# Stick-breaking scores without a mask product, and unsplit operands in 128-column products

## The chip, the cores and the metric

The kernel runs on one core of one Trainium2 chip. The metric is device time in microseconds of one execution; lower is better. A profile of one execution shows what each engine did: TensorE (PE, with its weight loads as PEld), VectorE (DVE), ScalarE (ACT), GpSimd (POOL) and the DMA queues issued from SP and ACT.

## What is computed

Two identical layers over 512 tokens of width 1024. Each layer norms the residual, projects it once, feeds four groups of heads, gates each group, concatenates, projects back, norms and adds. The two groups that matter here, cut to the core of the reference:

```python
def retention(q, k, v):                      # 4 heads of 128, chunks of 128
    q, k = apply_rope(q), apply_rope(k) * d ** -0.5
    scores = einsum('bcnhd,bcmhd->bchnm', qc, kc) * intra      # causal decay
    y_intra = einsum('bchnm,bcmhe->bcnhe', scores, vc)
    y = y_intra + y_inter                    # then a norm over each head
...
def stick_breaking(q, k, v):                 # 4 heads of 128, blocks of 128 queries
    logits = einsum('bthd,bshd->bhts', q_blk, k) * scale
    causal = key_pos[None, :] < q_pos[:, None]
    log_beta = log_sigmoid(logits)
    log_1mb = where(causal, log_sigmoid(-logits), 0.0)
    tail = cumsum(log_1mb, axis=3, reverse=True) - log_1mb
    w = where(causal, exp(log_beta + tail), 0.0)
    return einsum('bhts,bshd->bthd', w, v)
```

The other two groups are a state-space mixer (SSD) and a read of 256 memory tokens. Everything is float32.

## The kernel before

A product whose operands are float32 is written as three products in a reduced form (float32r): each operand is kept as a high part and a low part (a `Pair`: `h` and `l`, made by `split`, lines 287 to 290: a ScalarE copy that rounds, then a VectorE subtraction), and `mm3` (line 283) issues high by high, high by low and low by high into the same PSUM bank. Some products of the SSD group take float32 operands as they are, in one `mm` (lines 902 to 905, 919 and 936 to 945).

Weights come in blocks of 1 MB, are split on arrival (`w_prefetch`) and taken by the projections in a fixed order. The projections give banks of 128 features by 512 tokens (`proj_b`) or 128 tokens by 256 or 512 features (`proj_a`, `proj_v`). The work is written as a sequence of units; `defer` puts the later steps of a head some units behind, so that a head's chain of small steps runs beside the projections of later heads. The framework orders the instructions of each engine at compile time and places the semaphores; only the beginning (`start`) keeps the order in which it is written.

Stick-breaking, one head (`sb_head`, line 648): query and key are projected and split; for each of four blocks of 128 queries, t = 0 to 3, the scores against the first 128 (t + 1) keys are three split products and a fourth, bf16 product of an identity with a table of 0 and -1e30, which masks the keys at or after the query on the diagonal block (line 660; both bf16 tables lie in `b16`, filled at the end of `start`, and `b16` also feeds the warm-up products). Then, on the score tile `u`: absolute value, exponential and logarithm on ScalarE, a maximum and addition on VectorE, a reversed running sum on VectorE (the scan, line 666), a subtraction, and a last exponential, which gives the weights. `sb_head2` transposes the weights on TensorE (line 680) and splits them; `sb_head3` multiplies them with the values. The score tiles `w` lie in buffers of the tag "r" (9 of them); most others have the tag "s" (33) or "y" (16).

Retention, one head (`ret_head`, line 735): query and key are projected, rotated (`rope`) and split; for each chunk c of 128 keys the scores against the queries from that chunk on are one `mm3` of 512 - 128 c columns, which is split again, and the diagonal block of both parts is cleared by a GpSimd select (line 747). `ret_head2` multiplies them with the values, again with 512 - 128 c columns for chunk c. The values come from `ret_v`, one tile of 128 tokens each, shifted, scaled and split.

So for t = 0 in stick-breaking's scores, for the last j in its value product, and for the last c in both of retention's products the moving operand has 128 columns.

Of the kernel before, what the change touches and what calls it, by code (L numbers as in the profile page):

```python
# [16 lines left out]
P = 128  # L17
# [109 lines left out]
    return np.ascontiguousarray(t.T.reshape(KC, P, -1).transpose(1, 0, 2).reshape(P, -1))  # L127


CO = dict(ident=0, tri=128, ones=256, neg=384, cos=512, sin=1024, ginv=1536, reps=1552)  # L130
NCON = 1552 + 64
RP, RJ = 32, 16


def shape_constants():
    c = np.zeros((P, NCON), np.float32)
    i = np.arange(P)
    c[:, 0:128] = np.eye(P)
    c[:, 128:256] = i[:, None] <= i[None, :]
    c[:, 256:384] = 1.0  # L140
    c[:, 384:512] = np.where(i[None, :] >= i[:, None], NEG, 0.0)
    inv = np.float32(10000.0) ** (-np.arange(0, HD, 2, dtype=np.float32) / np.float32(HD))
    ang = (np.arange(SEQ, dtype=np.float32)[:, None] * inv[None, :].astype(np.float32)).T
    c[:, 512:1024] = np.concatenate([np.cos(ang), np.cos(ang)])
    c[:, 1024:1536] = np.concatenate([np.sin(ang), -np.sin(ang)])
# [3 lines left out]
    c[:, 1536:1552] = gi.reshape(NT, P, HEADS).transpose(1, 0, 2).reshape(P, 16)  # L149
    er = EPS * gam[None, :] ** (-2.0 * m[:, None])  # L150
    c[:RP, 1552:1616] = er.reshape(RP, RJ, HEADS).transpose(0, 2, 1).reshape(RP, HEADS * RJ)
    return c


# [16 lines left out]
class Builder:  # L171
# [4 lines left out]
    def __init__(self, tc, pools, args, taps=None):  # L176
        self.tc, self.nc = tc, tc.nc
        self.a = args
        self.taps = taps or {}
        self.fix, self.slots, self.small, self.wp, self.ps, self.dr = pools  # L180
        self.n = self.unit = 0
        self.todo, self.tanhs = [], []
        self.C = self.fixed(NCON + DEPTH * NPAR, F32, "consts")
        self.b16 = self.fixed(2 * P, BF16, "b16")
        self.onesr = self.fixed(P, F32R, "onesr")
        self.mhalf = self.fixed(RJ, F32, "mhalf")
        self.eps4 = self.fixed(RJ, F32, "eps4")
        self.nc.gpsimd.memset(self.mhalf[:], -0.5)
        self.nc.gpsimd.memset(self.eps4[:], EPS)

# [382 lines left out]
    def scaled_pair(self, b, scale):  # L573
# [2 lines left out]
        self.nc.vector.scalar_tensor_tensor(out=q.l, in0=b, scalar=scale, in1=q.hf, op0=ALU.mult, op1=ALU.subtract)  # L576
        return q

    @staticmethod
    def vcols(v, t, h):  # L580

        o = 256 * (t % 2) + HD * (h % 2)
        p = v[t // 2][h // 2]
        return p.h[:, o:o + HD], p.l[:, o:o + HD]
# [46 lines left out]
    def sb_v(self, l):  # L631
        nc = self.nc
        banks = self.proj_a(extra=SSD_H, turns=l == 0)
        if l:
            self.behind(self.turn[3], self.marks[1])
        first = [Pair(self), Pair(self)]
        u = self.tiny(32)
        uv = u.rearrange("p (h c) -> p c h", c=4)
        bias = self.par(l, "dtb", 0, 32).rearrange("p (h c) -> p c h", c=4)
        for t, b in enumerate(banks):  # L640
            p, c = first[t // 2], slice(256 * (t % 2), 256 * (t % 2) + 256)
            self.split(b[:, :256], p.h[:, c], p.l[:, c], p.hf[:, c])
            nc.vector.tensor_add(uv[:, t], b[:, 256:256 + SSD_H], bias[:, t])
        self.defer(1, self.dt_chain, l, u)
        second = [self.pair(b) for b in self.proj_a()]
        return [[first[i], second[i]] for i in range(2)]

    def sb_head(self, h, v):
        nc = self.nc
        q = self.scaled_pair(self.proj_b(), SCALE)  # L650
        k = self.pair(self.proj_b())
        w = [t[:, c] for t, c in self.packed([P * (t + 1) for t in range(NT)], lambda: self.buf(tag="r"))]
        for t in range(NT):
            n = P * (t + 1)
            ts = slice(P * t, P * t + P)
            b = self.mx()[:, :n]
            self.mm(b, q.h[:, ts], k.h[:, :n], True, False)
            self.mm(b, q.h[:, ts], k.l[:, :n], False, False)
            self.mm(b, q.l[:, ts], k.h[:, :n], False, False)
            self.mm(b[:, P * t:n], self.b16[:, 0:P], self.b16[:, P:2 * P], False, True)  # L660
            u = w[t]
            nc.scalar.activation(u, b, AF.Abs)
            self.act1(u, u, AF.Exp, scale=-1.0)
            self.act1(u, u, AF.Ln, bias=1.0)
            nc.vector.scalar_tensor_tensor(out=u, in0=b, scalar=0.0, in1=u, op0=ALU.max, op1=ALU.add)
            nc.vector.tensor_tensor_scan(out=u[:, ::-1], data0=u[:, ::-1], data1=u[:, ::-1], initial=0.0,
                                         op0=ALU.add, op1=ALU.bypass)
            nc.vector.tensor_sub(u, b, u)
            self.act1(u, u, AF.Exp)
        y = self.buf(tag="y")  # L670
        self.defer(4, self.sb_head2, h, v, w, y)
        return y

    def sb_head2(self, h, v, w, y):
        nc = self.nc
        wT = self.pairs_packed([SEQ - P * j for j in range(NT)])
        for j in range(NT):
            b = self.mx()
            for t in range(j, NT):
                nc.tensor.transpose(b[:, P * t:P * t + P], w[t][:, P * j:P * j + P], self.con("ident", P))  # L680
            self.split(b[:, P * j:], *wT[j])
        self.defer(2, self.sb_head3, h, v, wT, y)

    def sb_head3(self, h, v, wT, y):
# [24 lines left out]
    def rope(self, b):  # L709
        nc = self.nc  # L710
        cos, sin = self.con("cos", SEQ), self.con("sin", SEQ)
        A, B = self.buf(), self.buf()
        nc.vector.tensor_tensor(out=B[0:64], in0=b[64:128], in1=sin[64:128], op=ALU.mult)
        nc.vector.tensor_tensor(out=B[64:128], in0=b[0:64], in1=sin[0:64], op=ALU.mult)
        nc.vector.tensor_tensor(out=A, in0=b, in1=cos, op=ALU.mult)
        nc.vector.tensor_add(A, A, B)
        return self.pair(A)

    def row_rstd(self, row, eps):

# [14 lines left out]
    def ret_head(self, h, v):  # L735
        nc = self.nc
        q = self.rope(self.proj_b())
        k = self.rope(self.proj_b())
        sc = self.pairs_packed([SEQ - P * c for c in range(NT)])
        for c in range(NT):  # L740
            n = SEQ - P * c
            cs, ms = slice(P * c, SEQ), slice(P * c, P * c + P)
            b = self.mx()[:, :n]
            self.mm3(b, k.h[:, ms], k.l[:, ms], q.h[:, cs], q.l[:, cs], True, True)
            self.split(b, *sc[c])
            for d in (sc[c][0][:, :P], sc[c][1][:, :P]):
                nc.gpsimd.affine_select(out=d, in_=d, pattern=[[1, P]], compare_op=ALU.is_ge, fill=0.0, base=0, channel_multiplier=-1)  # L747
        y = self.buf(tag="y")
        self.defer(4, self.ret_head2, h, v, sc, y)
# [340 lines left out]
    def start(self):  # L1090
# [123 lines left out]
```

## Time and profile before

| | us |
|---|---|
| median of 3 runs | 954.48 (954.02 to 954.70) |
| the profiled execution | 954.77 |
| span of the profiled execution, first to last instruction | 953.0 |

The span is what the profile's views cover; 1.8 us of the execution lie around it. The granted TensorE clock was 0.998 of full speed over the span. How to read the rows that follow in the prediction: a group's row gives the line of the listing, the engine, the operation, output and inputs by the program's names, shapes and count, and after the bar the busy time in us and the mean of one in ns, then the idle time before. A row of the timeline gives start and duration in us; consecutive equal instructions are merged into one row with a count. TensorE's durations overlap, since products are pipelined. Most products lie in helper functions, so their line is 281 throughout, and the names of the operands tell them apart: `pj<-hTh,wh` is a projection, `mx<-s,s` an attention product, `mx<-b` the bf16 product.

### The profile page before, as it was taken

The numbers are of one execution on the slowest core, as the hardware profiler recorded it, in microseconds if no ns is written. First come the engines' busy times: TensorE is split into PE (matmuls) and PEld (weight loads), VectorE is DVE, ScalarE is ACT, GpSimd is POOL, SyncE is SP. The second block draws the span as 40 slices with busy tenths as digits, with TensorE's granted clock in tenths as the row PEclk, the third lists the DMA queues.
The fourth block names the chain that finished last, engine by engine and source line by source line (L and its number), as shares of the span: only waits on it lengthen the run. The fifth ranks groups of instructions, "written<-read, shape, count | busy, mean of one in ns | idle before, by whom it ended". The sixth has DMA issues, their size and how long they took to land.

```text
span 953.0 us, 12669 instructions
## 1 busy us (share of the span) xinstructions
PE 944.9 (99%) x4863; PEld 797.0 (84%) x4863; DVE 654.5 (69%) x1052; ACT 455.5 (48%) x840; POOL 102.0 (11%) x160
## 2 busy tenths in 40 slices
PE   9999999999999999999999999999999999999997
PEld 7998888888888888888899888888888888888885
DVE  5765577867878786854487465769777878767443
ACT  7544575543555342643465345655444544435341
POOL 1100000001231201100040000000003410102001
PEclk9999999999999999999999999999999999999999
DMA  9442211222232523344345221103222343223502
GB/s 339 144 159 86 89 45 45 89 89 89 97 103 100 166 89 122 123 154 144 117 172 189 90 89 62 72 1 133 85 76 80 137 140 127 99 75 116 193 29 88
DMA packets 26732, 105.76 MB, mean 111 GB/s; under 512 B 4144, under 2 KB 4400, under 8 KB 17456
## 3 DMA queue, kind: packets, MB, share of 16 engines
q10 hardware_dynamic: 10224, 73.44, 22.1%
q1 hardware_dynamic: 16448, 31.52, 10.0%
q8 instruction: 38, 0.62, 0.3%
q14 instruction: 22, 0.18, 0.1%
HBM read 100.63 MB, written 4.28 MB: 110 GB/s over the span
## 4 chain that ended last, share of the span: by engine, by line
PE 98%; DMA 1%; DVEq 0%; SPq 0%; ACT 0%; issue 0%; POOLq 0%; POOL 0%; ACTq 0%; DVE 0%
PE pj L281 72%; PE mx L281 23%; PE mx L680 1%; DMA mem<-memT 1%; PE mx L619 1%; PE mx L469 1%; PE mx L890 0%; PE mx L910 0%; DVEq L1210 0%; POOLq L1210 0%; ACT s L1058 0%; ACT s L512 0%; SPq L495 0%; SPq L343 0%; SPq L1094 0%
## 5 line engine op out<-in xcount | busy, mean ns | idle before, releaser
L281 PE MATMUL pj<-hTh,wh 128*128 128x512 f32 x704 | 277.1, 394 | 0.0
L281 PE MATMUL pj<-hTh,wl 128*128 128x512 f32 x704 | 276.5, 393 | 0.0
L281 PE MATMUL pj<-hTl,wh 128*128 128x512 f32 x704 | 276.3, 392 | 0.0
L290 DVE TENSOR_TENSOR wl<-raw,wh 128x1024 fp32r<-128x1024 f32 (+2 forms) x155 | 183.7, 1190 | 123.3 <-ACT wh L289 119.3
L289 ACT CAST wh<-raw 128x1024 fp32r<-128x1024 f32 (+2 forms) x155 | 157.9, 1024 | 191.8 <-PE pj L281 153.0
L281 PEld LDWEIGHTS pj<-hTh,wl 128*128 128x128 f32 x704 | 132.4, 188 | 26.8
L281 PEld LDWEIGHTS pj<-hTl,wh 128*128 128x128 f32 x704 | 132.4, 188 | 26.4
L281 PEld LDWEIGHTS pj<-hTh,wh 128*128 128x128 f32 x704 | 132.4, 188 | 26.2
L281 PE MATMUL pj<-wh,s 128*128 128x512 f32 x320 | 97.7, 391 | 0.0
L281 PE MATMUL mx<-s,s 128*128 128x128 f32 (+4 forms) x616 | 94.8, 309 | 0.0
L281 PEld LDWEIGHTS mx<-s,s 128*128 128x128 f32 (+1 forms) x616 | 84.5, 178 | 11.8 <-issue 2.4
L281 PE MATMUL mx<-wh,s 128*128 128x512 f32 x256 | 79.1, 389 | 0.0
L281 PEld LDWEIGHTS pj<-wh,s 128*128 128x128 f32 x320 | 59.7, 188 | 12.5
L747 POOL TENSOR_SCALAR_AFFINE_SELECT s<-s 128x128 fp32r<-128x128 f32 x64 | 20.5, 354 | 395.0 <-DVE s L290 395.0
L290 DVE TENSOR_TENSOR s<-mx,s 128x512 fp32r<-128x512 f32 (+2 forms) x86 | 41.8, 515 | 27.8 <-ACT s L289 27.8
L281 PE MATMUL pj<-wl,s 128*128 128x512 f32 x160 | 60.2, 390 | 0.0
L281 PEld LDWEIGHTS mx<-wh,s 128*128 128x128 f32 x256 | 48.1, 188 | 9.9
L290 DVE TENSOR_TENSOR s<-y,s 128x512 fp32r<-128x512 f32 x64 | 41.2, 686 | 19.7 <-ACT s L289 14.0
L289 ACT CAST s<-mx 128x512 fp32r<-128x512 f32 (+2 forms) x86 | 36.5, 456 | 37.0 <-PE mx L281 23.0
L289 ACT CAST s<-y 128x512 fp32r<-128x512 f32 x64 | 36.5, 617 | 29.4 <-PE mx L281 22.0
L281 PE MATMUL mx<-wl,s 128*128 128x512 f32 x128 | 49.6, 389 | 0.0
L281 PE MATMUL pj<-wl,hTh 128*128 128x256 f32 (+2 forms) x144 | 48.7, 338 | 0.0
(169 smaller groups left out, 1289.2 us busy)
## 6 DMA issues: line engine op xcount, KB each, us to landing
raw<-wts ACTq DMA_DIRECT2D x69, 1024.0 KB, 4.8
s<-x SPq DMA_DIRECT2D x24, 256.0 KB, 4.0
s<-acs SPq DMA_DIRECT2D x16, 256.0 KB, 6.4
raw<-wts SPq DMA_DIRECT2D x3, 1024.0 KB, 7.7
r<-row SPq DMA_DIRECT2D x12, 256.0 KB, 3.3
s<-acs SPq DMA_DIRECT2D x16, 128.0 KB, 5.9
x<-s SPq DMA_DIRECT2D x8, 256.0 KB, 2.0
out<-s SPq DMA_DIRECT2D x8, 256.0 KB, 2.0
```

The source lines that it names most:

```text
L281: return self.nc.tensor.matmul(out, lhsT, rhs, start=start, stop=stop)
L289: self.nc.scalar.copy(h, src)
L290: self.nc.vector.tensor_sub(l, src, hf)
L469: x = self.nc.tensor.transpose(b[:, P * j:P * j + P], hn[i][:, P * j:P * j + P], self.con("ident", P))
L619: nc.tensor.transpose(b[:, P * t:P * t + P], w[t // 2][:, o:o + P], self.con("ident", P))
L680: nc.tensor.transpose(b[:, P * t:P * t + P], w[t][:, P * j:P * j + P], self.con("ident", P))
L747: nc.gpsimd.affine_select(out=d, in_=d, pattern=[[1, P]], compare_op=ALU.is_ge, fill=0.0, base=0, channel_multiplier=-1)
```

## The change

1. The mask's product goes. The scan gets a constant table `run` (0 where a running sum starts, 1 elsewhere) as its first input, and multiplies the state by it before it adds: what lies at or after the query doesn't reach the sum. The weights of the diagonal block that should be zero are cleared by a GpSimd select after the last exponential.
2. Four 128-column triples a head become one product of float32 operands as they are. For that the first 128 columns of the scaled query and of the key are copied unsplit (`first_chunk`), the values' last chunk (`f` in `sb_v`) and the last transposed weights are kept unsplit, retention's rotated query and key are kept (`p.f`), and the last value tile of `ret_v` and the last score tile aren't split.
3. Buffers: the score tiles move to the tag "s", the last value tile of retention to "y". The constants get 384 columns more, and are loaded 3 and 12.6 tiles of 128 columns at a time instead of 4 and 8.6.

```diff
-            self.mm(b, q.h[:, ts], k.h[:, :n], True, False)
-            self.mm(b, q.h[:, ts], k.l[:, :n], False, False)
-            self.mm(b, q.l[:, ts], k.h[:, :n], False, False)
-            self.mm(b[:, P * t:n], self.b16[:, 0:P], self.b16[:, P:2 * P], False, True)
+            if t == 0:
+                self.mm(b, q.f, k.f, True, True)
+            else:
+                self.mm(b, q.h[:, ts], k.h[:, :n], True, False)
+                self.mm(b, q.h[:, ts], k.l[:, :n], False, False)
+                self.mm(b, q.l[:, ts], k.h[:, :n], False, True)
...
-            nc.vector.tensor_tensor_scan(out=u[:, ::-1], data0=u[:, ::-1], data1=u[:, ::-1], initial=0.0,
-                                         op0=ALU.add, op1=ALU.bypass)
+            nc.vector.tensor_tensor_scan(out=u[:, ::-1], data0=run[:, SEQ - n:][:, ::-1], data1=u[:, ::-1], initial=0.0,
+                                         op0=ALU.mult, op1=ALU.add)
             nc.vector.tensor_sub(u, b, u)
             self.act1(u, u, AF.Exp)
+            d = u[:, P * t:]
+            nc.gpsimd.affine_select(out=d, in_=d, pattern=[[-1, P]], compare_op=ALU.is_gt, fill=0.0, base=0, channel_multiplier=1)
...
+    def first_chunk(self, b, scale, out):
+        self.nc.scalar.activation(out, b[:, :P], AF.Copy, scale=scale)
+        return out
...
-        w = [t[:, c] for t, c in self.packed([P * (t + 1) for t in range(NT)], lambda: self.buf(tag="r"))]
+        w = [t[:, c] for t, c in self.packed([P * (t + 1) for t in range(NT)], self.buf)]
...
-            self.split(b[:, P * j:], *wT[j])
+            if j == NT - 1:
+                nc.scalar.copy(f, b[:, P * j:])
+            else:
+                self.split(b[:, P * j:], *wT[j])
...
-            self.mm3(b[:, c], *self.vcols(v, j, h), wT[j][0], wT[j][1], j == 0, j == NT - 1)
+            if j == NT - 1:
+                self.mm(b[:, c], v[2][:, HD * h:HD * h + HD], f, False, True)
+            else:
+                self.mm3(b[:, c], *self.vcols(v, j, h), wT[j][0], wT[j][1], j == 0, False)
...
-            vt = self.buf(tag="r")
+            vt = self.buf(tag="y" if t == NT - 1 else "r")
...
-            out.append(self.pair(vt))
+            out.append(vt if t == NT - 1 else self.pair(vt))
...
-            self.mm3(b, k.h[:, ms], k.l[:, ms], q.h[:, cs], q.l[:, cs], True, True)
-            self.split(b, *sc[c])
-            for d in (sc[c][0][:, :P], sc[c][1][:, :P]):
+            if c == NT - 1:
+                self.mm(b, k.f[:, ms], q.f[:, cs], True, True)
+                sc.append(k.f[:, :P])
+                nc.scalar.copy(sc[c], b)
+            else:
+                self.mm3(b, k.h[:, ms], k.l[:, ms], q.h[:, cs], q.l[:, cs], True, True)
+                self.split(b, *sc[c])
+            for d in (sc[c],) if c == NT - 1 else (sc[c][0][:, :P], sc[c][1][:, :P]):
...
-            self.mm3(b[:, P * c:], v[c].h[:, o], v[c].l[:, o], sc[c][0], sc[c][1], c == 0, c == NT - 1)
+            if c == NT - 1:
+                self.mm(b[:, P * c:], v[c][:, o], sc[c], False, True)
+            else:
+                self.mm3(b[:, P * c:], v[c].h[:, o], v[c].l[:, o], sc[c][0], sc[c][1], c == 0, False)
...
-        nc.sync.dma_start(self.C[:, 0:4 * P], self.a["consts"][:, 0:4 * P])
+        nc.sync.dma_start(self.C[:, 0:3 * P], self.a["consts"][:, 0:3 * P])
...
-        nc.sync.dma_start(self.C[:, 4 * P:NCON], self.a["consts"][:, 4 * P:NCON])
+        nc.sync.dma_start(self.C[:, 3 * P:NCON], self.a["consts"][:, 3 * P:NCON])
...
-        nc.vector.tensor_copy(self.b16[:, 0:P], self.con("ident", P))
-        nc.vector.tensor_copy(self.b16[:, P:2 * P], self.con("neg", P))
```

More of the change, by code (lines that the diff above doesn't have):

```diff
@@ L127, in features_first @@
     return np.ascontiguousarray(t.T.reshape(KC, P, -1).transpose(1, 0, 2).reshape(P, -1))
-CO = dict(ident=0, tri=128, ones=256, neg=384, cos=512, sin=1024, ginv=1536, reps=1552)
-NCON = 1552 + 64
+CO = dict(ident=0, tri=128, ones=256, run=384, cos=896, sin=1408, ginv=1920, reps=1936)
+NCON = 1936 + 64
 RP, RJ = 32, 16
@@ L140, in shape_constants @@
     c[:, 256:384] = 1.0
-    c[:, 384:512] = np.where(i[None, :] >= i[:, None], NEG, 0.0)
+    c[:, 384:896] = np.arange(512)[None, :] < 383 + i[:, None]
     inv = np.float32(10000.0) ** (-np.arange(0, HD, 2, dtype=np.float32) / np.float32(HD))
     ang = (np.arange(SEQ, dtype=np.float32)[:, None] * inv[None, :].astype(np.float32)).T
-    c[:, 512:1024] = np.concatenate([np.cos(ang), np.cos(ang)])
-    c[:, 1024:1536] = np.concatenate([np.sin(ang), -np.sin(ang)])
+    c[:, 896:1408] = np.concatenate([np.cos(ang), np.cos(ang)])
+    c[:, 1408:1920] = np.concatenate([np.sin(ang), -np.sin(ang)])
     gam = 1.0 - 2.0 ** (-5.0 - np.arange(HEADS, dtype=np.float64))
@@ L148, in shape_constants @@
     gi = gam[None, :] ** (-m[:, None]) * SCALE
-    c[:, 1536:1552] = gi.reshape(NT, P, HEADS).transpose(1, 0, 2).reshape(P, 16)
+    c[:, 1920:1936] = gi.reshape(NT, P, HEADS).transpose(1, 0, 2).reshape(P, 16)
     er = EPS * gam[None, :] ** (-2.0 * m[:, None])
-    c[:RP, 1552:1616] = er.reshape(RP, RJ, HEADS).transpose(0, 2, 1).reshape(RP, HEADS * RJ)
+    c[:RP, 1936:2000] = er.reshape(RP, RJ, HEADS).transpose(0, 2, 1).reshape(RP, HEADS * RJ)
     return c
@@ L183, in __init__ @@
         self.C = self.fixed(NCON + DEPTH * NPAR, F32, "consts")
+        self.mhalf = self.fixed(RJ, F32, "mhalf")
+        self.eps4 = self.fixed(RJ, F32, "eps4")
         self.b16 = self.fixed(2 * P, BF16, "b16")
         self.onesr = self.fixed(P, F32R, "onesr")
-        self.mhalf = self.fixed(RJ, F32, "mhalf")
-        self.eps4 = self.fixed(RJ, F32, "eps4")
         self.nc.gpsimd.memset(self.mhalf[:], -0.5)
@@ L644, in sb_v @@
         self.defer(1, self.dt_chain, l, u)
-        second = [self.pair(b) for b in self.proj_a()]
-        return [[first[i], second[i]] for i in range(2)]
+        f = self.buf(tag="r")
+        nc.scalar.copy(f[:, :256], banks[3][:, :256])
+        banks = self.proj_a()
+        second = [self.pair(b) for b in banks]
+        nc.scalar.copy(f[:, 256:], banks[1][:, 256:])
+        return [first[0], second[0]], [first[1], second[1]], f
     def sb_head(self, h, v):
         nc = self.nc
-        q = self.scaled_pair(self.proj_b(), SCALE)
-        k = self.pair(self.proj_b())
-        w = [t[:, c] for t, c in self.packed([P * (t + 1) for t in range(NT)], lambda: self.buf(tag="r"))]
+        f = self.buf(3 * P)
+        b = self.proj_b()
+        q = self.scaled_pair(b, SCALE)
+        q.f = self.first_chunk(b, SCALE, f[:, :P])
+        b = self.proj_b()
+        k = self.pair(b)
+        k.f = self.first_chunk(b, 1.0, f[:, P:2 * P])
+        w = [t[:, c] for t, c in self.packed([P * (t + 1) for t in range(NT)], self.buf)]
+        run = self.con("run", SEQ)
         for t in range(NT):
@@ L665, in sb_head, with sb_head2 @@
             nc.vector.scalar_tensor_tensor(out=u, in0=b, scalar=0.0, in1=u, op0=ALU.max, op1=ALU.add)
-            nc.vector.tensor_tensor_scan(out=u[:, ::-1], data0=u[:, ::-1], data1=u[:, ::-1], initial=0.0,
-                                         op0=ALU.add, op1=ALU.bypass)
+            nc.vector.tensor_tensor_scan(out=u[:, ::-1], data0=run[:, SEQ - n:][:, ::-1], data1=u[:, ::-1], initial=0.0,
+                                         op0=ALU.mult, op1=ALU.add)
             nc.vector.tensor_sub(u, b, u)
             self.act1(u, u, AF.Exp)
+            d = u[:, P * t:]
+            nc.gpsimd.affine_select(out=d, in_=d, pattern=[[-1, P]], compare_op=ALU.is_gt, fill=0.0, base=0, channel_multiplier=1)
         y = self.buf(tag="y")
-        self.defer(4, self.sb_head2, h, v, w, y)
+        self.defer(4, self.sb_head2, h, v, w, f[:, 2 * P:], y)
         return y
-    def sb_head2(self, h, v, w, y):
+    def sb_head2(self, h, v, w, f, y):
         nc = self.nc
-        wT = self.pairs_packed([SEQ - P * j for j in range(NT)])
+        wT = self.pairs_packed([SEQ - P * j for j in range(NT - 1)])
         for j in range(NT):
@@ L716, in rope @@
         nc.vector.tensor_add(A, A, B)
-        return self.pair(A)
+        p = self.pair(A)
+        p.f = A
+        return p
     def row_rstd(self, row, eps):
@@ L738, in ret_head @@
         k = self.rope(self.proj_b())
-        sc = self.pairs_packed([SEQ - P * c for c in range(NT)])
+        sc = self.pairs_packed([SEQ - P * c for c in range(NT - 1)])
         for c in range(NT):
```

4 lines of the change are left out of this document (2 added, 2 removed).

## The prediction

> **What bounds the kernel now.** I read the page's totals first, then the chain of work that ended last, then the list of waits restricted to TensorE.
>
> ```profile
> span 953.0 us, 12669 instructions
> PE 944.9 (99%) x4863; PEld 797.0 (84%) x4863; DVE 654.5 (69%) x1052; ACT 455.5 (48%) x840; POOL 102.0 (11%) x160
> PE 98%; DMA 1%; DVEq 0%; SPq 0%; ACT 0%; issue 0%; POOLq 0%; POOL 0%; ACTq 0%; DVE 0%
> PE mx L281 <- POOL b L193: 1.2, 1, 1.2
> PE pj L281 <- ACT s L512: 0.6, 1, 0.6
> ```
>
> The reader is to see three things. TensorE has something in flight for 99% of the span, the chain runs through TensorE for 98% of it, and the two waits in the last rows, 1.8 us together, are all that this list has for TensorE's products, both in the first 12 us. So a microsecond of TensorE work removed is a microsecond off the end, as long as nothing else becomes late. A busy share hides pipelining, so TensorE work is priced below by the distance between starts, not by durations.
>
> The change touches mostly the stick-breaking stretch, about 118 to 197 us in layer 0 and again in layer 1. The table by stretches (length; busy time of PE, weight loads, DVE, ACT, POOL) says how much room the others have there:
>
> ```profile
> 118.00:145.00 27.00, 27.00 (x134) 21.99 (x134) 20.39 (x33) 20.15 (x45) 0.00 (x0) 1.00 0.12 41
> 145.00:175.00 30.00, 30.00 (x154) 24.57 (x154) 19.66 (x41) 16.61 (x41) 0.00 (x0) 1.00 0.11 36
> 175.00:197.00 22.00, 22.00 (x112) 18.41 (x111) 19.67 (x38) 12.38 (x23) 0.00 (x0) 1.00 0.42 144
> ```
>
> Of 79 us TensorE is busy for all, VectorE for 59.7, ScalarE for 49.1, GpSimd for none.
>
> **The step of one matmul.** From the chain in order of time, and from TensorE's timeline around one plain triple of 128-column split products:
>
> ```profile
> 395.35 40.59 PE pj L281 x179
> ```
> ```profile
> 253.84 0.39 PE L281 MATMUL pj<-hTl,wh 128*128 128x512 f32 x1
> 254.07 0.44 PE L281 MATMUL mx<-s,s 128*128 128x128 f32 x3
> 254.35 0.44 PE L281 MATMUL pj<-hTh,wl 128*128 128x512 f32 x1
> 254.63 0.40 PE L281 MATMUL pj<-hTh,wh 128*128 128x512 f32 x1
> ```
>
> A 512-column product steps by 40.59/179 = 0.227 us. From 253.84 to 254.63 are 0.79 us, which hold two such steps and the triple, so the triple costs 0.79 - 0.454 = 0.336 us, 0.112 a piece. That is half a 512-column step for a quarter of the columns.
>
> **Unsplit operands.** Does the trace show a 128-column float32 product that isn't split? Yes, in the SSD mixer:
>
> ```profile
> 309.98 0.39 PE L281 MATMUL pj<-hTh,wl 128*128 128x512 f32 x1
> 310.21 1.05 PE L281 MATMUL mx<-s,s 128*128 128x128 f32 x8
> 311.10 0.49 PE L910 MATMUL mx<-consts,s 128*128 128x128 f32 x3
> 311.35 0.49 PE L281 MATMUL pj<-hTh,wh 128*128 128x512 f32 x1
> 311.67 0.39 PE L281 MATMUL pj<-hTl,wh 128*128 128x512 f32 x1
> ```
> ```profile
> L281 PE MATMUL mx<-s,s 128*64 128x128 f32 x128 | 8.8, 279 | 0.0
> ```
>
> The program issues four products there (line 905 has one per chunk) and the trace records eight. The last row confirms the factor: the SSD diagonal issues 2 layers x 2 groups x 2 halves x 4 chunks x 2 heads = 64 of them, and 128 are recorded. So one unsplit product is two passes. From 309.98 to 311.67 are 1.69 us, less two 512 steps 1.236, for eleven passes (three are transposes): 0.112 each. An unsplit product costs 0.225 us against 0.336 for the triple: 0.111 saved. Neither end of the run shows a price for going from split to unsplit operands.
>
> How many: per head the first score tile and the last value product of stick-breaking, and the last score tile and the last value product of retention. Four, times 4 heads, times 2 layers: 32. **32 x 0.111 = 3.6 us.**
>
> **The mask's product.** It is the bf16 product at the end of each score tile, 32 in all. Its smallest and its largest setting, from TensorE's timeline:
>
> ```profile
> 135.46 0.39 PE L281 MATMUL pj<-hTl,wh 128*128 128x512 f32 x1
> 135.69 0.44 PE L281 MATMUL mx<-s,s 128*128 128x128 f32 x3
> 135.98 0.23 PE L281 MATMUL mx<-b 128*128 128x128 bf16 x1
> 136.02 0.47 PE L281 MATMUL pj<-hTh,wl 128*128 128x512 f32 x1
> 136.33 0.39 PE L281 MATMUL pj<-hTh,wh 128*128 128x512 f32 x1
> ```
> ```profile
> 139.54 0.40 PE L281 MATMUL pj<-hTh,wh 128*128 128x512 f32 x1
> 139.78 0.86 PE L281 MATMUL mx<-s,s 128*128 128x512 f32 x3
> 140.48 0.23 PE L281 MATMUL mx<-b 128*128 128x128 bf16 x1
> 140.52 0.47 PE L281 MATMUL pj<-hTl,wh 128*128 128x512 f32 x1
> 140.83 0.39 PE L281 MATMUL pj<-hTh,wl 128*128 128x512 f32 x1
> ```
>
> First: 0.87 us less two steps and the triple (0.454 + 0.336) leaves 0.08. Second: 1.29 less five steps (1.135) leaves 0.155. Part of it is the delayed step behind the mask (0.31 instead of 0.227). I take the middle, 0.118, since the four sizes are equally frequent: **32 x 0.118 = 3.8 us**, with ends 2.6 and 5.0. The 37 other bf16 products are the warm-up and stay.
>
> **What is added elsewhere, and what covers it.**
>
> ```profile
> L289 ACT CAST s<-mx 128x128 fp32r<-128x128 f32 x16 | 4.3, 269 | 6.4 <-PE mx L680 4.1 <-PE mx L281 2.3
> L290 DVE TENSOR_TENSOR s<-mx,s 128x128 fp32r<-128x128 f32 x16 | 4.5, 282 | 0.4 <-ACT s L289 0.4
> L747 POOL TENSOR_SCALAR_AFFINE_SELECT s<-s 128x128 fp32r<-128x128 f32 x64 | 20.5, 354 | 395.0 <-DVE s L290 395.0
> ```
> ```profile
> L666 DVE TENSOR_TENSOR_SCAN r<-r x32: 414/819/1217, 126.7 to 652.5; 128x128 f32<-128x128 f32 x8, 128x256 f32<-128x256 f32 x8, 128x384 f32<-128x384 f32 x8, 128x512 f32<-128x512 f32 x8
> ```
>
> ScalarE: first_chunk copies 128 columns twice a head, 8 x 0.27 = 2.2 us a layer in the stretch, and two value copies of 256 columns before it (twice that row, about 0.5 each, an estimate). 51.3 of some 76 us is no bound. VectorE: the 16 subtractions of the second row go (4.5 us), and with the last value tile of retention one 512-column split a layer. The scan keeps its form and columns; its operations become multiply and add and its first input another tensor, a form that this trace doesn't have. I take the durations of its row (shortest, median, longest in ns: 0.82 us at the median, 16 x 0.82 = 13.1 us a layer); the lower end is a plain subtraction of the same size (0.68 below, instead of 1.21 for 512 columns), the upper end a rival. GpSimd: 32 selects come, 8 go; at 0.35 us that is 5.6 us a layer in a stretch where its queue is empty, so nothing is queued behind them. Their own wait is for the last exponential, and the transposes wait for them. The tightest place is the last tile of layer 0's last head (VectorE, ScalarE, TensorE timelines):
>
> ```profile
> 187.51 0.68 DVE L668 TENSOR_TENSOR r<-mx,r 128x512 f32<-128x512 f32 x1
> 188.23 0.63 ACT L258 ACTIVATE r<-r 128x512 f32<-128x512 f32 x1 [0.90 <-DVE r L668]
> 191.34 0.63 PE L680 MATMUL mx<-consts,r 128*128 128x128 f32 x4
> ```
>
> The exponential ends at 188.86 and the next transposes of four start at 191.34: 2.5 us of slack for a 0.35 us step. Without that cover the price is at most 8 x 0.35 = 2.8 us. A select may also hold VectorE up, as SSD's selects do:
>
> ```profile
> L875 DVE TENSOR_TENSOR s<-s,t x16: 679/694/1118, 276.3 to 788.9; 128x512 f32<-128x512 f32 x16
> consts<-consts SPq DMA_DIRECT2D x1, 552.0 KB, 8.1
> ```
>
> The same subtraction takes 679 to 1118 ns, so 0.44 us at worst, 16 a layer: 7 us of VectorE in 16 idle ones. Nothing. The second constants' load grows by 512 columns, from 552 to 808 KB, and the first shrinks by 128. The first scan reads the new table at 126.7, long after the start; the weight load queued next on SP comes at most 3.8 us later (256/552 of 8.1). I cost it at nothing; if that weight block is just in time, up to 3.8 us. Two casts at the end of the start go, off TensorE's path. The larger pool moves (score tiles from the 9 r to the 33 s buffers, one value tile to y) issue nothing.
>
> **The sum.** 954.77 us of the profiled execution (span 953.0 and 1.8 around it) - 3.6 - 3.8 = 947.4. That execution was 0.3 over the median, 954.48, so I predict **947.1 us**. With the mask's ends (2.6 and 5.0) the forecast runs from 945.9 to 948.3, and 0.6 more for small reorderings: 948.9.
>
> **A rule against the change.** If columns alone set the step, 128 of them would be a quarter of 0.227, 0.057; the triple would cost 0.17 and the exchange for two passes of 0.112 would lose 0.055, 32 times 1.8 us; the mask would be worth 32 x 0.057 = 1.8 us. Net nothing: about 954.5. The rows at 253.84 speak against it (0.336), but those triples could owe it to their neighbours. [...]
>
> **Rivals.**
> 1. Columns alone count, as just worked out: no change, 954.5 us. 4 in 100.
> 2. The stretch closes up only in part. Counting by whole heads, the s buffers hold at once 8 value tiles, 12 transposed pairs of two heads, 4 to 8 query and key tiles, now 6 score tiles and 4 of the new f: 34 to 38 against 33. Tiles freed piece by piece make that less, and TensorE has value projections to run meanwhile. If half of the gain is lost in waits: 950.8 us. 12 in 100.
> 3. VectorE becomes the bound of the stretch because the new scan is slower. The stretch shrinks to 79 - 4 x (0.47 + 0.22) = 76 us; VectorE has 59.7 and the scans are 13.1 of it. Slower than before it gets from 79 us on: 19.3 more, or 12.4 with the selects' hold of 7 at its worst, so from a scan about twice as long. At three times (26.2 more), with those 7, it is 93 us, 14 a layer over the old 79, and retention's 16 x 0.111 come off: 954.5 + 28 - 1.8, about 981 us. For it: the form is new. Against: the step per element, 1.21 us for 512 columns, is nearly twice a subtraction's (0.68), so a feedback from element to element seems paid for. [...] 4 in 100.
>
> **Chances.** Forecast 0.80 (945.9 to 948.9), rival 2 0.12, rivals 1 and 3 0.04 each. For 8 in 10 with the mask's ends and a part of rival 2 the range is 945.9 to 949.8. 0.2% (1.9 us) is about what a measurement of this kernel tells from no change; forecast and rival 2 are both faster by more: 0.92, same 0.04, slower 0.04.
>
> **What would show it.** Right: TensorE 99% busy again with some 4863 - 32 - 32 = 4799 records, no waits of TensorE beyond the first 12 us, 128-column unsplit groups at 0.225 us, the scan's row at 1.21 us, the first stretch about 3 us shorter in each layer and each retention head 0.2 shorter. Wrong: idle time before TensorE in the stick-breaking stretch, released by GpSimd (select) or VectorE (scan); a step above 0.112 for the new passes; a constants' load that delays the first weight blocks.

## The result and the profile after

| | before | changed |
|---|---|---|
| median of 6 runs each, us | 954.34 (954.02 to 954.70) | 947.72 (947.45 to 949.76) |
| the profiled execution, us | 954.77 | 947.90 |
| its span, us | 953.0 | 946.2 |

The ratio is 0.9932, interval 0.9923 to 0.9942. The prediction said 947.1 us, 945.9 to 949.8.

The page of the changed kernel (span, busy time by engine, chain of waits by engine):

```profile
span 946.2 us, 12624 instructions
PE 937.7 (99%) x4799; PEld 792.6 (84%) x4799; DVE 649.6 (69%) x1032; ACT 459.6 (49%) x858; POOL 112.9 (12%) x184
PE 98%; DMA 1%; DVEq 0%; ACT 0%; SPq 0%; issue 0%; POOLq 0%; POOL 0%; ACTq 0%; DVE 0%
```

The list of TensorE's waits (what waits, for whom; us in total, times, longest):

```profile
PE mx L281 <- POOL b L193: 1.2, 1, 1.2
PE pj L281 <- ACT s L512: 0.8, 1, 0.8
```

TensorE has 4863 - 64 = 4799 records, is busy 99% again, bounds the chain as before, and its two waits are the two of the start. The stick-breaking stretch of layer 0, now 118 to 194 us (columns as in the prediction):

```profile
118.00:145.00 27.00, 27.00 (x128) 22.58 (x127) 18.75 (x32) 19.07 (x46) 3.43 (x6) 1.00 0.22 79
145.00:173.00 28.00, 28.00 (x141) 23.55 (x140) 22.61 (x46) 16.90 (x42) 2.01 (x6) 1.00 0.01 1
173.00:194.00 21.00, 21.00 (x106) 17.54 (x106) 16.96 (x27) 13.97 (x27) 1.47 (x4) 1.00 0.42 150
```

The reader is to see that TensorE fills every microsecond of a stretch that is 3 us shorter, while GpSimd has got 6.9 us of work in it. By the starts of equal projection products, layer 0 has gained 2.6 us when the stretch ends (204 us of before) and 0.6 more behind retention, 0.16 a head; layer 1 2.7 and 0.6.

**Start and layers apart.** Executions of one kernel differ by up to 2.6 us (954.13 to 956.74 for the kernel before, beside e1 to e4), and the traces show where: between 7 and 20 us, while the first weights arrive. So the runs are compared below by their traces too. "Start" is how much later than in the trace of before the projection product begins that stands there at 22.99 us; "layers" is the rest, from that product to the last one. Three traces of the changed kernel give start -0.36, +1.14 and 0.00, but layers -6.49, -6.46 and -6.48 us. A difference of 0.05 us in the layers can be read this way (of the kernel before there is one trace, which all have in common); a median can't show it.

A part of the late starts can be named. In the six traces that start 0.96 to 1.49 us late, the granted TensorE clock is 0.50 to 0.55 between 11.0 and 14.2 us, and 1.00 there in all others. Here are the changed kernel's first trace and that of e3 (the clock is the figure behind the five engines; PE stands first, with 27 records and 16):

```profile
11.00:14.20 3.20, 3.20 (x27) 3.20 (x28) 2.29 (x3) 2.57 (x3) 0.00 (x0) 1.00 1.03 397
11.00:14.20 3.20, 3.20 (x16) 3.20 (x17) 1.86 (x4) 2.13 (x3) 0.00 (x0) 0.55 1.02 390
```

e3 has 11 records fewer there, of 27 that take the 3.20 us: 1.3 us of work, an estimate from these two rows. Why the clock falls in some executions isn't shown.

| run | median us | ratio, interval | start | layers |
|---|---|---|---|---|
| changed kernel | 947.72 | 0.9932, 0.9923 to 0.9942 | -0.36 | -6.49 |
| e1_mask_alone | 952.30 | 0.9965, 0.9953 to 0.9978 | -0.62 | -3.55 |
| e2_exchange_alone | 952.97 | 0.9969, 0.9958 to 0.9980 | +1.12 | -2.62 |
| e3_after_again | 949.42 | 0.9932, 0.9920 to 0.9945 | +1.14 | -6.46 |
| e4_unsplit_256 | 953.73 | 0.9984, 0.9975 to 0.9993 | +0.96 | -1.39 |
| e5_no_select | 947.89 | 0.9927, 0.9914 to 0.9941 | -0.26 | -6.48 |
| e6_selects_x8 | 947.77 | 0.9931, 0.9917 to 0.9944 | -0.52 | -6.48 |
| e7_states_split | 949.98 | 0.9944, 0.9931 to 0.9956 | +1.37 | -6.15 |
| e8_unsplit_256_r | 949.12 | 0.9937, 0.9922 to 0.9952 | +1.49 | -5.61 |
| e9_s_28 | 953.25 | 0.9977, 0.9966 to 0.9987 | +1.38 | -1.77 |
| e10_s_24 | 994.24 | 1.0404, 1.0377 to 1.0431 | +0.11 | +33.65 |
| e11_states_two | 948.50 | 0.9929, 0.9917 to 0.9942 | +0.25 | -6.85 |
| e12_after_third | 948.02 | 0.9920, 0.9907 to 0.9934 | 0.00 | -6.48 |

The kernel before ran beside them: medians 954.86 (e1 to e4), 954.75 (e5 to e8) and 955.76 us (e9 to e12). One of e2's seven executions took 3359.5 us; the median of the other six is 952.46, and the ratio goes by them.

**The prices in the changed trace.** TensorE's timeline (start, duration, instruction, count), priced as in the prediction, from the 512-column step ahead of a group to the second one behind it, less two steps of 0.227:

```profile
138.61 0.40 PE L281 MATMUL pj<-hTh,wh 128*128 128x512 f32 x1
138.85 0.52 PE L281 MATMUL mx<-s,s 128*128 128x256 f32 x3
139.20 0.40 PE L281 MATMUL pj<-hTl,wh 128*128 128x512 f32 x1
139.43 0.39 PE L281 MATMUL pj<-hTh,wl 128*128 128x512 f32 x1
...
140.88 0.40 PE L281 MATMUL pj<-hTh,wh 128*128 128x512 f32 x1
141.12 0.85 PE L281 MATMUL mx<-s,s 128*128 128x512 f32 x3
141.81 0.39 PE L281 MATMUL pj<-hTl,wh 128*128 128x512 f32 x1
142.04 0.39 PE L281 MATMUL pj<-hTh,wl 128*128 128x512 f32 x1
...
249.46 0.39 PE L281 MATMUL pj<-hTh,wl 128*128 128x512 f32 x1
249.69 0.38 PE L281 MATMUL mx<-s,s 128*128 128x128 f32 x2
249.83 0.48 PE L281 MATMUL pj<-hTh,wh 128*128 128x512 f32 x1
250.14 0.40 PE L281 MATMUL pj<-hTl,wh 128*128 128x512 f32 x1
```

The 512-column scores are the counterpart of the prediction's second mask row: 1.16 us from 140.88 to 142.04 now, 1.29 then, so that mask was worth 0.13. The 256-column scores cost 0.82 - 0.454 = 0.366; the one group of this kind in before, with its mask, costs 0.486: 0.12. The pair at 249.69 is an unsplit product alone: 0.68 - 0.454 = 0.226, as predicted (0.225). The step behind it is 0.31 (249.83 to 250.14); behind a split triple it was 0.28 (254.35 to 254.63 in the prediction).

Two other rows that the prediction asked for, the scan by its line (shortest, median and longest in ns) and the selects by groups:

```profile
L683 DVE TENSOR_TENSOR_SCAN s<-consts,s x32: 410/818/1310, 127.8 to 646.3; 128x128 f32<-128x128 f32 x8, 128x256 f32<-128x256 f32 x8, 128x384 f32<-128x384 f32 x8, 128x512 f32<-128x512 f32 x8
```
```profile
L688 POOL TENSOR_SCALAR_AFFINE_SELECT s<-s 128x128 f32<-128x128 f32 x32 | 14.9, 465 | 292.0 <-ACT s L258 291.7
```

The scan's median is 818 ns (819 before): multiply and add cost it what add and bypass did. Its longest is 1310 ns (1217 before), and a select took 465 ns in the mean, a third more than the 354 taken. The two belong together: 19 of the 32 selects take 292 to 294 ns, the others up to 1337, and the five scans that are longer than their like, by 0.05 to 0.10 us, all begin while a select is running. The longest one of layer 0:

```profile
132.96 0.66 POOL L688 TENSOR_SCALAR_AFFINE_SELECT s<-s 128x128 f32<-128x128 f32 x1 [1.59 <-ACT s L258]
133.38 1.31 DVE L683 TENSOR_TENSOR_SCAN s<-consts,s 128x512 f32<-128x512 f32 x1
```

### The profile page after: what moved, and what is told of

Its sections match the earlier page's. It is cut to its first block, busy times and chain, and to the rows that moved or that the text cites. A ratio compares the mean times of both kernels' runs of the same rounds, so it can differ in the third digit from the quotient of the medians.

```text
span 946.2 us, 12624 instructions
## 1 busy us (share of the span) xinstructions
PE 937.7 (99%) x4799; PEld 792.6 (84%) x4799; DVE 649.6 (69%) x1032; ACT 459.6 (49%) x858; POOL 112.9 (12%) x184
## 4 chain that ended last, share of the span: by engine, by line
PE 98%; DMA 1%; DVEq 0%; ACT 0%; SPq 0%; issue 0%; POOLq 0%; POOL 0%; ACTq 0%; DVE 0%
PE pj L281 73%; PE mx L281 23%; PE mx L699 1%; PE mx L469 1%; PE mx L624 1%; DMA mem<-memT 1%; PE mx L925 0%; PE mx L945 0%; DVEq L1243 0%; ACT s L1093 0%; POOLq L1243 0%; ACT s L512 0%; SPq L343 0%; SPq L1129 0%; POOL t L439 0%
## 5 line engine op out<-in xcount | busy, mean ns | idle before, releaser
L281 PE MATMUL mx<-s,s 128*128 128x256 f32 (+4 forms) x536 | 85.1, 317 | 0.0
L281 PEld LDWEIGHTS mx<-s,s 128*128 128x128 f32 (+1 forms) x536 | 73.3, 176 | 11.2 <-issue 2.4
L281 PEld LDWEIGHTS pj<-wh,s 128*128 128x128 f32 x320 | 59.6, 188 | 12.6
L290 DVE TENSOR_TENSOR s<-mx,s 128x512 fp32r<-128x512 f32 (+2 forms) x70 | 37.6, 568 | 23.8 <-ACT s L289 23.8
L258 ACT ACTIVATE s<-s 128x384 f32<-128x384 f32 (+3 forms) x96 | 41.3, 475 | 20.0 <-DVE s L685 19.7
L688 POOL TENSOR_SCALAR_AFFINE_SELECT s<-s 128x128 f32<-128x128 f32 x32 | 14.9, 465 | 292.0 <-ACT s L258 291.7
L281 PE MATMUL pj<-wh,hTh 128*128 128x256 f32 (+2 forms) x144 | 48.4, 336 | 0.0
```

Of the source, the lines that this page charges most:

```text
L258: i = self.nc.scalar.activation(out, in_, func, **k)
L281: return self.nc.tensor.matmul(out, lhsT, rhs, start=start, stop=stop)
L290: self.nc.vector.tensor_sub(l, src, hf)
L688: nc.gpsimd.affine_select(out=d, in_=d, pattern=[[-1, P]], compare_op=ALU.is_gt, fill=0.0, base=0, channel_multiplier=1)
```

## The experiments

### The two halves

e1 removes the mask's product alone; all 128-column products stay split. Its main edit against the changed kernel (both halves keep the score tiles in the tag s):

```diff
-            if t == 0:
-                self.mm(b, q.f, k.f, True, True)
-            else:
-                ...
+            self.mm3(b, q.h[:, ts], q.l[:, ts], k.h[:, :n], k.l[:, :n], True, True)
```

e2 exchanges the 128-column products alone; the mask's product stays. Its edit of the scores against the kernel before:

```diff
-            self.mm(b, q.h[:, ts], k.h[:, :n], True, False)
...
+            if t == 0:
+                self.mm(b, q.f, k.f, True, False)
...
             self.mm(b[:, P * t:n], self.b16[:, 0:P], self.b16[:, P:2 * P], False, True)
```

> The mask's product goes, with the new scan and the GpSimd selects; every 128-column product stays a triple of split products. Theory (TensorE's steps add up, all else is covered): the mask's 32 products are worth 2.6 to 5.0 us by the steps of before; after's trace shows that a lone triple keeps a part of the edge that was counted with the mask (700 ns where three steps are 681), so 3.1: 951.2 us, 950.7 to 951.7. Rival (columns alone set a step): 1.8 us, 952.5. Rival (the new scan or the selects cost time): not below 953.

> The 32 triples of 128 columns become unsplit products; the mask's product, the old scan and the old constants stay, no selects are added. Theory: 32 x 0.111 = 3.6 us off, 950.8, within 0.5; two passes of 0.112 us each in the trace. Rival (columns alone set a step): 1.8 us more, 956.1. The two halves together should give the whole: this gain and that of the mask alone add up to 6.6 us within 0.5.

> The changed kernel once more, to compare with in the same session and to see where its runs of 949 to 950 us come from. Theory: 947.6 us. If the later ones come from the beginning, a profiled run at 949 or more differs before 22 us of the span and nowhere after; if from the stick-breaking stretch, between 118 and 197 us.

In the layers the mask alone gave 3.55 us (predicted 3.8), the exchange alone 2.62 (predicted 3.6), both together 6.48. The halves sum to 6.17. (The medians, 952.30 and 952.97, lie above the expected 951.2 and 950.8; the start is in them.) To see where the exchange fell short, the time from each TensorE record's start to the next, summed by the columns of the moving operand (from the 320th projection product to the 3600th, us):

| columns | before | changed | mask alone | exchange alone |
|---|---|---|---|---|
| 128, float32 | 46.02 | 42.00 | 45.87 | 42.79 |
| 128, bf16 (the mask) | 1.26 | 0 | 0 | 1.16 |
| 256 and 384 | 71.00 | 70.09 | 70.46 | 70.62 |
| 512, not projections | 36.96 | 36.99 | 36.83 | 37.35 |
| 512, projections | 686.35 | 686.03 | 684.87 | 687.05 |
| others | 12.22 | 12.22 | 12.22 | 12.22 |

The mask's own steps are 1.26 of its 3.5 us; most of the rest was in the projections, which began late behind it. In the exchange alone, the smaller products shrink by 3.23 + 0.38 = 3.6 us, just the predicted sum, but the 512-column products take back 0.39 + 0.70. Behind an unsplit pair the first 512 step is 0.314 to 0.319, behind a split triple 0.280 to 0.292; that was inside the price of 0.225. What wasn't are the steps after it. Among 512 steps with a 512 step on either side the mean is 227.48 ns in before, 227.49 with the mask alone, 227.67 with the exchange alone and 227.64 in the changed kernel: 0.16 ns more on 2741 steps, 0.44 us. About 0.2 us of it lies in the second to fourth step behind a 128-column attention product (233.0, 233.2 and 233.1 ns at 24 places against 231.3, 230.7 and 228.4). The rest lies in the same stretches: taken by the times of before, the excess stands in 118 to 290 us (0.24) and 585 to 758 us (0.24), where the exchanged products are (0.03 each with the mask alone), while from 75 to 118 and from 340 to 480 us the means of before and of the changed kernel agree to 0.01 ns. So nearly all of it comes with the unsplit products, and not from another clock: in both traces 1.00 is granted in each of these four stretches. By which mechanism isn't settled.

A value product, at the end of a longer sequence, is worth a little less too. By the same pricing the last score tiles of retention save 0.110 to 0.118 and the first score tile alone 0.110, but the value products of stick-breaking 0.104 and those of retention 0.088 to 0.108 (1.908 to 1.800 or 1.820 for the sequence). One sequence of retention scores, first in before, then in the changed kernel (11 records now, 12 then):

```profile
212.24 0.39 PE L281 MATMUL pj<-hTl,wh 128*128 128x512 f32 x1
212.47 2.00 PE L281 MATMUL mx<-s,s 128*128 128x512 f32 x12
214.31 0.45 PE L281 MATMUL pj<-hTh,wl 128*128 128x512 f32 x1
214.60 0.40 PE L281 MATMUL pj<-hTh,wh 128*128 128x512 f32 x1
```
```profile
207.94 0.39 PE L281 MATMUL pj<-hTl,wh 128*128 128x512 f32 x1
208.16 1.95 PE L281 MATMUL mx<-s,s 128*128 128x512 f32 x11
209.87 0.48 PE L281 MATMUL pj<-hTh,wl 128*128 128x512 f32 x1
210.19 0.39 PE L281 MATMUL pj<-hTh,wh 128*128 128x512 f32 x1
```

2.36 - 2.25 = 0.11. Eight pieces of each kind, 8 x (0.110 + 0.114 + 0.104 + 0.095), make 3.4 us; less 0.44 that is 2.9, and measured are 6.48 - 3.55 = 2.93. The 0.31 by which the whole beats its halves is the first score tile: with a mask behind it the exchange takes the group from 0.412 to 0.336, without one from 0.336 to 0.226, and 8 x 0.034 = 0.27.

### The next size: 256 columns unsplit

e4 takes the second to last chunk of retention unsplit as well, 16 products of 256 columns; e8 is e4 with all value tiles in the tag r.

```diff
-            vt = self.buf(tag="y" if t == NT - 1 else "r")
+            vt = self.buf(tag="y" if t >= NT - 2 else "r")
...
-            if c == NT - 1:
+            if c >= NT - 2:
                 self.mm(b, k.f[:, ms], q.f[:, cs], True, True)
...
-            if c == NT - 1:
-                self.mm(b[:, P * c:], v[c][:, o], sc[c], False, True)
+            if c >= NT - 2:
+                self.mm(b[:, P * c:], v[c][:, o], sc[c], False, c == NT - 1)
```

> The changed kernel, and in retention the two 256-column products (scores of the third chunk, and its value product) unsplit as well: 16 triples of 256 columns become one unsplit product each. Theory (a split pass costs 0.112 us at 128 and 0.120 at 256 columns, an unsplit pass 0.112 and 0.216, so the exchange pays only where the split pass is bound by something other than its columns): each costs 0.432 for 0.360, 16 x 0.072 = 1.15 us slower, 948.8. Rival (three passes to two always save a third): 16 x 0.12 = 1.9 us faster, 945.7.

> The kernel of e4_unsplit_256 (256-column products unsplit too) with the unsplit value tiles of retention in buffers of the tag r, not y. Theory (the waits of 1.9 us twice a layer in e4 come from value tiles that wait for y buffers given out in program order, behind the stick-breaking heads' outputs, and meanwhile hold a projection bank each): the scaling of the last value tile comes by about 190 us, not 197 to 200; TensorE's waits on VectorE (line 740) go; of the 5.1 us that e4 lost only the 1.1 us of the dearer passes stays, so layers about 5.4 us below before, about 948.5 to 950.5 us. Rival (VectorE itself is late there): the same waits, 952 to 954 us.

e4 lost 5.1 us of the layers against the changed kernel, far more than the dearer products explain. TensorE's waits in e4 beyond the two of the start, and the line that scales retention's values into tiles of the tag y (starts of the first and the last):

```profile
PE pj L281 <- DVE s L740: 2.3, 2, 1.1
...
PE mx L281 <- ACT s L701: 0.8, 2, 0.4
```
```profile
L729 DVE TENSOR_SCALAR r<-pj,t,consts x16: 399/401/411, 154.8 to 632.0; 128x128 f32<-128x128 f32 x16
L729 DVE TENSOR_SCALAR y<-pj,t,consts x16: 397/402/404, 197.1 to 666.0; 128x128 f32<-128x128 f32 x16
```

The tiles of the tag r are scaled from 154.8 us on, those of the tag y only from 197.1. Until then each of the two holds one of the four projection banks, and a projection of retention finds none. The same line in the changed kernel, which has one such tile a layer (scaled from 198.3 us on, though its statistics are ready at 178.1), and in e8:

```profile
L729 DVE TENSOR_SCALAR y<-pj,t,consts x8: 402/404/408, 198.3 to 663.3; 128x128 f32<-128x128 f32 x8
```
```profile
L729 DVE TENSOR_SCALAR r<-pj,t,consts x32: 399/402/412, 155.3 to 646.9; 128x128 f32<-128x128 f32 x32
```

With the tag r the last scaling comes at 646.9, not 666.0, TensorE's list has the two waits of the start alone, and 4.2 of the 5.1 us come back. So it was the tag y that made the tiles late. That they stand there behind the outputs of the stick-breaking heads, which come before them in the program and are written at about 200 us, fits the times but wasn't tried by itself. The changed kernel has the same late tile, and one held bank in four costs it nothing. What is left, 6.48 - 5.61 = 0.87 us for 16 products, 0.054 each, is the price of 256 columns unsplit.

### The selects

e5 leaves the select on the stick-breaking weights out; e6 issues each eight times:

```diff
-            nc.gpsimd.affine_select(out=d, in_=d, pattern=[[-1, P]], compare_op=ALU.is_gt, fill=0.0, base=0, channel_multiplier=1)
+            for _ in range(8):
+                nc.gpsimd.affine_select(out=d, in_=d, pattern=[[-1, P]], compare_op=ALU.is_gt, fill=0.0, base=0, channel_multiplier=1)
```

> The changed kernel without the 32 GpSimd selects on the stick-breaking weights: the weights of keys at or after the query stay as the exponential leaves them. Theory (the selects are hidden: GpSimd's queue is empty there and the last exponential of a head ends 2.5 us before the transposes that read it): the layers, counted from the same projection product at 22 us to the end, stay within 0.3 us of the changed kernel's 6.5 us below before; about 947.5 to 949.5 us by how long the start takes. Rival (the selects are part of what the mask's removal gave less than counted, 3.56 instead of 3.8 us): the layers become 0.3 to 2.8 us shorter.

> The changed kernel with each of the 32 stick-breaking selects issued eight times over (the result is the same): 7 x about 0.4 = 2.8 us more on GpSimd between the last exponential of a tile and its transposes. By the slack of 2.5 us that the prediction read, the tightest place, the last head of a layer, is just missed: theory 0 to 0.5 us a layer, so 947.5 to 950.5 us, with a short wait of TensorE's transposes on GpSimd (line 692 or so) at the last head at most. Rival (no cover, each head's chain sets the end): 8 heads x 2.8 = 22 us, about 970.

```profile
L689 POOL TENSOR_SCALAR_AFFINE_SELECT s<-s 128x128 f32<-128x128 f32 x256 | 96.8, 401 | 220.3 <-ACT s L258 212.3
```

With none and with 256 of them (this row, of e6) the layers are the same to 0.01 us, -6.48. So the selects are covered even at 3.2 us instead of 0.47, and the 2.5 us read as slack at the tightest place in before were less than there is in the changed kernel. They do hold single scans up, as shown above; without them (e5) no scan takes over 1221 ns:

```profile
L683 DVE TENSOR_TENSOR_SCAN s<-consts,s x32: 412/820/1221, 127.9 to 646.2; 128x128 f32<-128x128 f32 x8, 128x256 f32<-128x256 f32 x8, 128x384 f32<-128x384 f32 x8, 128x512 f32<-128x512 f32 x8
```

In VectorE's busy time this is lost (649.6 us with 32 selects, 649.9 with none, 650.2 with 256), and at the end it costs nothing.

### The SSD states, the other way round

If 256 columns are dearer unsplit, the 12 state products of SSD, unsplit in both kernels, should gain from being split. e7 splits all of them (and their operands on arrival), e11 two of each three.

```diff
-            self.mm(b, bt[:, P * c:P * c + P], xds[c // 2][:, 256 * (c % 2):256 * (c % 2) + 256], True, True)
+            x, m, s = xds[c // 2], slice(P * c, P * c + P), slice(256 * (c % 2), 256 * (c % 2) + 256)
+            self.mm3(b, bt.h[:, m], bt.l[:, m], x.h[:, s], x.l[:, s], True, True)
```

> The changed kernel with the 12 state products of the SSD mixer that have 256 columns and unsplit operands written as three split products instead. Theory (an unsplit product is two passes, each 0.112 us at 128 columns but 0.216 at 256, so that at 256 columns the triple is the cheaper, by 0.43 - 0.36 = 0.07 us): 12 x 0.07 = 0.86 us shorter in the layers, 7.3 us below before; about 946.7 to 948.6 us. Rival (an unsplit product saves a pass at any size): 12 x 0.11 = 1.3 us slower, about 949 to 951.

> The changed kernel with two of each three 256-column state products of the SSD mixer as split triples (8 in all), the third unsplit as before. In e7_states_split the nine passes of a triple group cost 1.08 us against 1.30 for the six unsplit ones, as priced, but one half-width output product of SSD moved into the middle of the full-width ones there, and that group of 44 passes went from 3.78 to 4.33 us. Here the instruction order of those 44 is the one of the changed kernel. Theory (both prices are right): layers 8 x 0.07 = 0.6 us shorter than the changed kernel's, 7.0 to 7.1 below before, every group of 44 at 3.78 us; about 946.9 to 949 us by the start. Rival (the split's extra copies and subtractions are what cost the time in e7): layers 6.1 to 6.5 below before.

> The changed kernel once more, beside e11_states_two: layers 6.48 below before, 947.4 to 949.9 us by the start.

One group of three unsplit state products in the changed kernel:

```profile
311.25 0.39 PE L281 MATMUL pj<-hTh,wh 128*128 128x512 f32 x1
311.48 1.46 PE L281 MATMUL mx<-s,s 128*128 128x256 f32 x6
312.58 0.58 PE L281 MATMUL pj<-hTl,wh 128*128 128x512 f32 x1
313.00 0.39 PE L281 MATMUL pj<-hTh,wl 128*128 128x512 f32 x1
```

The groups cost what the theory says: three unsplit products 1.297 us (1.75 - 0.454) in the changed kernel, their nine split passes 0.479 + 0.603 = 1.082 in e7, and in e11 six split passes and one unsplit product 1.150. Yet e7's layers are 0.33 us longer, not 0.86 shorter. The group of SSD's output products behind the states, the first of four, in the changed kernel and in e7:

```profile
322.18 3.85 PE L281 MATMUL mx<-s,s 128*64 128x128 f32 x44
325.79 0.48 PE L281 MATMUL pj<-hTh,wh 128*128 128x512 f32 x1
```
```profile
323.70 4.40 PE L281 MATMUL mx<-s,s 128*64 128x128 f32 x44
327.85 0.47 PE L281 MATMUL pj<-hTh,wh 128*128 128x512 f32 x1
```

The same 44 records take 3.61 us there and 4.15 here. In the changed kernel they are 16 half-width records, 6 of full width, 16 and 6; in e7 one half-width product has moved in between the full-width ones. The starts in the changed kernel show why that costs: half-width records that go in pairs step by 0.110 us a pair (0.007 and 0.103), full-width ones by 0.112, but the steps at a change of width take 0.202 to 0.214, and the first half-width pair behind a change 0.160. By these steps a change from half to full width costs about 0.20 us (0.202 and 0.213 where 0.103 and 0.112 are usual) and one back 0.14 (0.205 for 0.112, and 0.160 for 0.110); why isn't shown. The moved product brings one more of each, 0.34, and it and the one that it leaves behind run without a partner, 0.11 each: 0.56, an estimate from these steps, where 0.54 were measured. Two of the four groups have it, and the 0.86 gained are more than gone.

e11 keeps the order of the 44 (3.78 us by the same pricing in every group) and has 0.36 us of the 0.59 that its groups save: its layers, -6.85, are the shortest of all, between theory (-7.0) and rival (-6.5). Where the rest went wasn't followed. Beside e12 this doesn't show in the medians, 948.50 against 948.02: the start decides there. No version here beats the changed kernel by more than a measurement tells.

### Fewer buffers of the tag s

Counted from the first write of a tile to its last read, the changed kernel fills at most 32 of its 33 s buffers at once in the stick-breaking stretches, before at most 25. Elsewhere the pool is fuller: towards the end of a layer (about 440 to 460 us) both kernels come to 33.

e9 has 28, e10 has 24:

```diff
-    SLOTS = {"s": 33, "y": 16, "r": 9}
+    SLOTS = {"s": 28, "y": 16, "r": 9}
```

> The changed kernel with 28 buffers of the tag s in place of 33. The trace of the changed kernel has at most 32 of them filled at once. Theory (the stretch had room, and TensorE has value projections to run while a head waits for a buffer): layers within 0.5 us of 6.5 below before, another order of TensorE's work, no waits. Rival (the prediction's second: the s buffers are what lets the stretch close up): over 2 us of TensorE waits in the two stretches, 949.5 us or more.

> The same with 24 buffers of the tag s. Both theories see it bind: the heads of the stretch run one behind the other, the projections run out, TensorE waits on the score tiles' chain. By the prediction's count (34 to 38 by whole heads) 24 are two thirds; I expect 5 to 25 us of TensorE waits in the two stretches. If there are under 1 us, the count of buffers plays no part in this change at all.

TensorE's waits in e9, those of over 0.5 us that the changed kernel doesn't have, then the largest in e10:

```profile
PE pj L281 <- DVE s L558: 1.6, 1, 1.6
...
PE pj L281 <- DVE s L740: 1.2, 2, 0.6
PE pj L281 <- DVE y L729: 0.6, 2, 0.3
```
```profile
PE mx L469 <- DVE s L460: 10.0, 3, 4.4
PE pj L281 <- ACT wh L289: 4.4, 5, 1.0
PE mx L281 <- ACT s L701: 4.1, 4, 1.7
PE mx L281 <- ACT s L581: 3.2, 2, 1.6
...
PE pj L281 <- DVE s L740: 1.2, 2, 0.6
```

My theory for e9 falls: 28 buffers cost 4.7 us of the layers, 3.4 of them in these waits. Half of that is where the stretch ends (a projection of retention waits for its bank twice a layer, at 201 and 220 us), the longest single one at the end of layer 0. By the starts of equal projection products 1.4 us are lost by 400 us, 1.9 at the end of layer 0 and 1.4 in layer 1. The 1.9 follow a stretch in which the kernel before comes to 33 buffers too, so they needn't be due to the change; the kernel before with 28 wasn't run. With 24 the two stretches wait for 8.5 us (the rows of L701, L581 and L740), as expected, and the rest of the 40 us is lost outside them, above all at the end of layer 0, where the weights come late and the rows of L469 stand; the granted clock is 0.95 in the mean from 480 to 515 us (1.00 from 118 to 194), and 0.986 over the span. So the second rival's mechanism is real. It just didn't decide at 33.

## Why the prediction was right, point by point

**TensorE bounds, and what it sheds comes off the end.** Right: 99% busy, chain 98%, no new wait, and the difference grows only where products were removed.

**The exchange, 3.6 us.** The mechanism and the price of one alone (0.225 against 0.336) were right, the term was too large: 2.93 us in the changed kernel, 2.62 alone. The step that failed is the pricing over two 512 steps and its sentence "Neither end of the run shows a price for going from split to unsplit operands". One end does: the 512 steps around the unsplit products are longer by 0.44 us in all, beyond the two steps that were priced, and the value products, at the end of a sequence, save less than a piece that stands alone (0.2 us). How the unsplit products lengthen steps further behind stays open.

**The mask, 3.8 us.** Measured alone 3.55. The middle of 0.08 and 0.155 was 0.118, measured 0.111 a piece.

**The rest at nothing.** Right, for each that was tried: the selects are covered at eight times their number, and the scan costs the same. The constants' larger load shows nowhere: e1 has it and starts 0.62 us early, e2 hasn't and starts 1.12 late. The price of one select was taken a quarter too low in the mean, without effect. That a select may hold VectorE up was right, and small: 0.05 to 0.10 us for five of 32 scans, where 0.44 a subtraction was allowed.

**The sum.** Predicted 7.4 us off the profiled execution's 954.77, and 0.3 more down to the median. The layers gave 6.48; the profiled execution's start happened to be 0.36 shorter. The median came out 0.6 us above the forecast: the exchange's 0.7 and the mask's 0.25, less what the start gave. That it lies so near is luck in part, for the median goes by how many executions start late: e3, the same kernel, has 949.42, and e12 948.02.

**The rivals.** The first, columns alone, falls with the pair at 0.226 and the triple's 0.336. The third falls with the scan's 818 ns, 819 before. Why a scan of 512 columns takes 1.21 us where a subtraction takes 0.68 isn't shown by any run; that a feedback is paid for was the author's estimate. The second didn't happen, but by a narrow margin: the forecast counted 34 to 38 tiles by whole heads, the trace has 32 in the stretches, and five buffers fewer would have cost 4.7 of the 6.5 us, some 2.8 of them outside the end of layer 0. Its 12 in 100 were not too many.

## What to carry to other kernels

Where a product is short, an unsplit one can be cheaper than three split ones, but price it at its own size: here 128 columns save 0.09 to 0.11 us each and 256 lose 0.05 to 0.07. Price a piece over several steps behind it, not two, since the products that follow were longer here by 0.44 us in all. Before tiles are moved to another pool, count its peak from the trace, and ask in which order that pool hands its buffers out: five s buffers, or one more tile in y, would have cost most of this gain.

## What the runs showed of the hardware

- An unsplit float32 product costs 0.226 us at 128 columns and 0.432 at 256 (1.297/3), nearly in proportion to its columns; a split pass costs 0.112 and 0.120 (1.082/9 in e7), hardly more for twice the columns. The trace records two passes for each unsplit product (six for the three at 311.48), so a pass of it costs 0.113 and 0.216. Why its cost nearly doubles with the columns and a split pass's doesn't, no run here shows.
- The step behind a 128-column product was 0.314 to 0.319 us when that was unsplit, bf16 or a transpose (0.312 to 0.324 there), and 0.280 to 0.292 behind a split triple.
- Two half-width products of SSD start 7 ns apart and together step by 0.110 us; a change from half to full width costs about 0.20 us and one back about 0.14, worked out from the steps in the changed kernel's trace (322.18 to 325.79 us).
- In the changed kernel's trace a GpSimd select and a VectorE scan that overlap can both be longer than their like: scans that begin during a select take up to 0.10 us more (1.31 for 1.21 us), and a select that begins 0.01 us behind a scan takes 1.03 us instead of 0.29. Without the selects (e5) no scan takes over 1.221 us.
